# A two-layer hybrid decoder trunk on one core: expert weights in pieces of 1536 columns, and no native float32 product in the small places

## The chip, the cores and the metric

The kernel runs on one core of one Trainium2 chip. The metric is the device time of one execution in microseconds (us). Engines are written as in the profile: PE is the matrix engine (PEld its loading of the stationary operand), DVE the vector engine, ACT the scalar engine, POOL the general-purpose engine, SP the engine whose queue issues the weight loads. A line such as L241 is line 241 of the kernel before.

## What is computed

Two layers over 256 tokens of width 1024, all float32. Each layer adds a mixer (gated delta rule heads, forgetting attention, pooling groups) and then a feed-forward part: dense in layer 0, and in layer 1 two of eight experts for each token. The change is in the last of these:

```
def swiglu(h, w_gate, w_up, w_down):
    return (jax.nn.silu(h @ w_gate) * (h @ w_up)) @ w_down

def moe_swiglu(h, router, w_gate, w_up, w_down):
    ...
    top_p, top_i = lax.top_k(probs, TOP_K)
    ...
    for e in range(N_EXPERTS):
        out = out + gates[:, e:e + 1] * swiglu(ht, w_gate[e], w_up[e], w_down[e])
```

Each expert has w_gate and w_up of 1024 x 1536 and w_down of 1536 x 1024, so 18.87 MB of weights an expert and 151 MB in all.

## The kernel before

The program runs four stages in a row: "mix0", "dense", "mix1" and "all" (the experts). In all of them weights stream from HBM in **pieces** (`piece`, L283): a DMA on SP's queue into a float32 buffer `raw`, a copy on ACT that rounds it to the float32r tile `whi` (L238), a subtraction on DVE that leaves the rest in the float32r tile `wlo` (L241). PE then makes a product of full precision out of several float32r products (`mm3`, L246: high x high, high x low, low x high). A `raw` buffer is free for the next load when DVE has written `wlo`; a pair `whi`, `wlo` is free when PE has made its last product with it.

The buffers are 1152 columns wide (PIECE, L55). Six `raw` buffers (L196) and four pairs (L197) serve all four stages; the expert stage has six more `raw` buffers in its own pool (`load`, L268, and L1329).

The expert stage first normalizes, routes and sorts: the experts get eight **places** by how many tokens they have (`places`). Places 2, 4 and 7 are **small** (SMALL, L41): at most 64 tokens, whose high and low parts lie side by side in the 128 columns of one stationary tile, so that two products (with `whi` and with `wlo`) do what `mm3` does with three. The other five places are **big**, with up to 128 tokens. For each place four **chunks** of 384 expert columns are worked through (`steps`, L1241): `gate_up` (L1151) makes two sums `ps_e` over eight k-blocks of 384 columns, `down` (L1191) transposes the result (`ps_ht`), splits it into `ehi`, `elo` and adds three k-blocks of 1024 columns into `ps_y`. After the last chunk of a place `finish` scales `ps_y` on ACT and DVE (`yh`, `yl`), and after places 1, 3, 5 and 7 `scatter` makes `ps_sc` and adds it to `xs` on DVE. `gather` (L1124) fetches the token columns of the next two places (`ps_ga`, `gThi`, `gTlo`).

A chunk's weights come in nine pieces before: three of gate, three of up (1152, 1152 and 768 columns, by `k_cuts`, L64) and three of down (1024 columns each). In a small place the 768-column piece of gate and of up is not split: `whole` (L277) loads it and PE multiplies the float32 `raw` tile itself, in native float32 (L1161 to L1165). So a small chunk has seven splits and a big one nine.

The order of instructions on each engine is set by the framework's scheduler from the program's priorities; pieces are put 2000 instructions ahead (AHEAD, L56) by `high_priority`. Each engine works through its own order strictly in turn.

Of the kernel before, what the change touches and what calls it, by code (L numbers as in the profile page):

```python
# [16 lines left out]
F32 = mybir.dt.float32  # L17
F32R = mybir.dt.float32r
# [7 lines left out]
D = 1024  # L26
# [9 lines left out]
NFC = 4  # L36
# [15 lines left out]
for _n, _c, _s in GROUPS:  # L52
    GOFF[_n], GCOLS[_n] = _o, _c
    _o += 8 * _c
PIECE = 1152  # L55
AHEAD = 2000  # L56
RING = 6
BANKS = {"mix0": {"A": 3, "D": 3, "F": 2}, "mix1": {"A": 3, "D": 3, "F": 2},
         "dense": {"A": 4, "D": 2, "F": 2}, "all": {"A": 2, "D": 4, "F": 2}}

OUT_ORDER = (3, 4, 5, 6, 7, 0, 1, 2)


def k_cuts(n):  # L64

    step = PIECE // n
    return [(a, min(8, a + step)) for a in range(0, 8, step)]


# [120 lines left out]
class Kernel:  # L190
    def __init__(self, ctx, tc, aps, out, dbg=None):
        self.tc, self.nc, self.d, self.out = tc, tc.nc, aps, out
        self.dbg = dbg
        pool = lambda n, b, **k: ctx.enter_context(tc.tile_pool(name=n, bufs=b, **k))
        self.cp = pool("const", 1)
        self.rp = pool("ring", RING)  # L196
        self.sp = pool("split", 4)  # L197
        self.big = pool("big", 2)
        self.sm = pool("small", 2)
        self.loads = self.more = 0  # L200
        self.guard = None
        self.phase_insts = []

# [61 lines left out]
            self.nc.sync.dma_start(self.dbg[name], ap)  # L265


    def load(self, ap, n):  # L268
        self.loads += 1
        if self.more and self.loads % (RING + self.more) >= RING:  # L270
            raw = self.wk.tile([128, PIECE], F32, tag="raw2", name="raw", bufs=self.more)
        else:
            raw = self.rp.tile([128, PIECE], F32, tag="raw", name="raw")
        self.nc.sync.dma_start(raw[:, :n], ap)
        return raw

    def whole(self, ap):  # L277

        n = ap.shape[1]
        with self.tc.high_priority(offset=AHEAD):  # L280
            return self.load(ap, n)[:, :n]

    def piece(self, ap):  # L283

        n = ap.shape[1]
        with self.tc.high_priority(offset=AHEAD):
            src = self.load(ap, n)[:, :n]
            hi = self.sp.tile([128, PIECE], F32R, tag="whi", name="whi")
            lo = self.sp.tile([128, PIECE], F32R, tag="wlo", name="wlo")
# [819 lines left out]
    def experts(self, over, xh, xl):  # L1109
# [81 lines left out]
        def down(p, fc, hh, py):  # L1191
            small = p in small_ones
# [8 lines left out]
                h1 = wk.tile([128, 3, 128], F32R, tag="ehi", name="ehi", bufs=2)  # L1201
                h2 = wk.tile([128, 3, 128], F32R, tag="elo", name="elo", bufs=2)
            self.hi_lo(h1, h2, ps[:, :3 * r].rearrange("p (j c) -> p j c", j=3))
            for j in range(3):
                wh, wl = self.piece(self.weights(p, fc, 2, j * D, j * D + D))
                for i in range(2):
                    c = slice(i * 512, i * 512 + 512)
                    first, last = fc == 0 and j == 0, fc == NFC - 1 and j == 2
                    if small:
                        x = h[:, j].rearrange("p i c -> p (i c)")  # L1210
                        self.mm(py[i], x, wh[:, c], first, False)
                        self.mm(py[i], x, wl[:, c], False, last)
                    else:
                        self.mm3(py[i], h1[:, j], h2[:, j], wh[:, c], wl[:, c], first, last)

        def finish(p, py):
            sl, tk = info
# [99 lines left out]
            self.store()  # L1317


def build(tc, aps, out, dbg=None, stop=None):  # L1320
    with ExitStack() as ctx:
        k = Kernel(ctx, tc, aps, out, dbg)
        k.setup()
        for name, part in (("mix0", lambda: k.mixer(0)), ("dense", k.dense), ("mix1", lambda: k.mixer(1)), ("all", k.moe)):
            if stop == "setup":
                break
            k.n4 = 10 if name == "all" else 3
            k.banks = BANKS[name]
            k.more = 12 - RING if name == "all" else 0  # L1329
            with tc.tile_pool(name=name, bufs=1) as k.wk, tc.tile_pool(name=name + "_ps", bufs=1, space=PSUM) as k.pp:  # L1330
                part()
            if stop == name:
                break
        if not stop or stop == "all":
            return
        k.store()


# [10 lines left out]
```

## Time and profile before

| what | value |
|---|---|
| median of 3 runs | 986.07 us (984.82 to 990.4) |
| the profiled execution, its own time | 986.57 us |
| its span, first to last instruction | 984.8 us |
| busy share of the span | PE 94%, PEld 84%, DVE 75%, ACT 63%, POOL 13% |
| mean granted PE clock | 0.981 of full speed |
| pieces of expert weights | 128 of 576 KB, 96 of 512 KB, 64 of 384 KB; median 5.8 to 6.0 us from issue to landing |

Busy shares are means over four stages. The expert stage takes the last part of the span: its first product `ps_e` starts at 544 us, the last `wlo` ends at 970.6 us. In the table of windows a stretch is one place, cut at the start of the place's first `wlo` on DVE; each row gives the busy time of the engines in it, with the number of instructions in brackets. A busy PE is modelled from pipelined products, so that back-to-back starts and not the busy time tell whether PE waits.

### The profile page before, as it was taken

The page shows a single profiled execution, that of the slowest core. Times are in us where ns is not written, and L with a number is a line of the kernel's source. Part 1 is how long each engine was busy: PE and PEld are TensorE (multiplying, and loading weights), DVE is VectorE, ACT ScalarE, POOL GpSimd, SP SyncE. Part 2 cuts the span into 40 slices and gives each one's busy share as a digit, 9 for nine tenths or more (in the row PEclk, how much of TensorE's full clock was granted, in tenths as well). Part 3 has the DMA queues.
Part 4 walks back from the last instruction along what each step waited for, and adds up shares of the span by engine and source line. Part 5 has one row for each costly group of instructions (what it writes and reads, how often), then busy time and mean ns, then how long its engine had stood idle before and what let it go on. Part 6 is the DMA issues. An engine that isn't in the chain of part 4 may idle for free.

```text
span 984.8 us, 17576 instructions
## 1 busy us (share of the span) xinstructions
PE 926.0 (94%) x6483; PEld 825.3 (84%) x6483; DVE 733.9 (75%) x1036; ACT 624.0 (63%) x987; POOL 129.3 (13%) x196
## 2 busy tenths in 40 slices
PE   6998998999999989889994999999999899999996
PEld 6987776999999979888773999987899788998874
DVE  5877657655555567857658587999899898998895
ACT  6754545544444457565635388887887688777773
POOL 2596100000000023891002000000000000000000
PEclk9999999999999999999997799999999999999999
DMA  9534113666666637342135299999999999998991
GB/s 353 159 99 129 45 44 126 206 191 190 181 184 191 170 113 234 109 121 76 41 104 210 82 366 323 351 366 370 394 350 378 353 338 363 377 347 320 328 401 49
DMA packets 61983, 224.78 MB, mean 228 GB/s; under 512 B 6896, under 2 KB 7152, under 8 KB 61888
## 3 DMA queue, kind: packets, MB, share of 16 engines
q1 hardware_dynamic: 61344, 221.62, 64.7%
q0 software_dynamic: 544, 1.94, 0.6%
q8 instruction: 53, 0.87, 0.4%
q14 instruction: 42, 0.34, 0.1%
HBM read 222.49 MB, written 1.05 MB: 227 GB/s over the span
## 4 chain that ended last, share of the span: by engine, by line
PE 75%; DVE 9%; POOL 6%; DMA 3%; ACT 2%; issue 2%; SPq 0%; DVEq 0%; ACTq 0%; POOLq 0%
PE ps_e L244 23%; PE ps_gu L244 13%; PE ps_y L244 11%; PE ps_dn L244 6%; PE ps_out L244 4%; DVE wlo L241 3%; DMA raw<-moe 2%; PE ps_ga L244 2%; PE ps_fq L244 2%; PE ps_zabf L244 2%; POOL U L576 2%; PE ps_o L244 1%; PE ps_p L244 1%; POOL tmp L574 1%; PE ps_s L244 1%
## 5 line engine op out<-in xcount | busy, mean ns | idle before, releaser
L241 DVE TENSOR_TENSOR wlo<-raw,whi 128x1024 fp32r<-128x1024 f32 (+3 forms) x394 | 478.7, 1240 | 138.1 <-ACT whi L238 135.1
L238 ACT ACTIVATE whi<-raw 128x1024 fp32r<-128x1024 f32 (+3 forms) x394 | 412.5, 1066 | 185.9 <-PE ps_e L244 51.6
L244 PE MATMUL ps_e<-wlo,gThi 128*128 128x384 f32 x464 | 160.8, 347 | 4.4 <-DVE wlo L241 4.4
L244 PE MATMUL ps_e<-whi,gThi 128*128 128x384 f32 x464 | 156.8, 344 | 1.2 <-ACT whi L238 1.2
L244 PE MATMUL ps_e<-whi,gTlo 128*128 128x384 f32 x320 | 108.0, 339 | 0.0
L244 PE MATMUL ps_gu<-hThi,whi 128*128 128x256 f32 x352 | 99.8, 283 | 1.3 <-DVE hTlo L241 1.3
L244 PE MATMUL ps_gu<-hThi,wlo 128*128 128x256 f32 x352 | 99.4, 283 | 0.0
L244 PE MATMUL ps_gu<-hTlo,whi 128*128 128x256 f32 x352 | 99.4, 282 | 0.0
L244 PEld LDWEIGHTS ps_e<-wlo,gThi 128*128 128x128 f32 x464 | 88.4, 191 | 9.6 <-DVE wlo L241 6.8
L244 PEld LDWEIGHTS ps_e<-whi,gThi 128*128 128x128 f32 x464 | 88.2, 191 | 4.6 <-ACT whi L238 1.6
L244 PE MATMUL ps_y<-wlo,ehi 128*128 128x512 f32 x192 | 73.4, 401 | 1.0 <-DVE wlo L241 1.0
L244 PEld LDWEIGHTS ps_gu<-hThi,whi 128*128 128x128 f32 x352 | 67.3, 191 | 2.5 <-DVE hTlo L241 1.5
L244 PEld LDWEIGHTS ps_gu<-hTlo,whi 128*128 128x128 f32 x352 | 67.3, 191 | 1.0
L244 PEld LDWEIGHTS ps_gu<-hThi,wlo 128*128 128x128 f32 x352 | 67.3, 191 | 0.0
L244 PE MATMUL ps_y<-whi,ehi 128*128 128x512 f32 x192 | 65.7, 407 | 1.3 <-DVE ehi L241 1.3
L244 PEld LDWEIGHTS ps_e<-whi,gTlo 128*128 128x128 f32 x320 | 61.1, 191 | 0.6
L244 PE MATMUL ps_y<-whi,elo 128*128 128x512 f32 x120 | 46.5, 391 | 0.0
L244 PEld LDWEIGHTS ps_y<-whi,ehi 128*128 128x128 f32 x192 | 36.1, 190 | 9.6 <-DVE ehi L241 2.1
L244 PEld LDWEIGHTS ps_y<-wlo,ehi 128*128 128x128 f32 x192 | 36.3, 190 | 9.1 <-DVE wlo L241 1.8
L244 PE MATMUL ps_dn<-whi,fhi 128*128 128x512 f32 x88 | 35.0, 398 | 0.0
L244 PE MATMUL ps_e<-raw,gThi 128*128 128x384 f32 x96 | 34.9, 486 | 0.0
L244 PE MATMUL ps_dn<-wlo,fhi 128*128 128x512 f32 x88 | 34.8, 395 | 0.0
(394 smaller groups left out, 1791.8 us busy)
## 6 DMA issues: line engine op xcount, KB each, us to landing
raw<-moe SPq DMA_DIRECT2D x128, 576.0 KB, 6.0
raw<-moe SPq DMA_DIRECT2D x96, 512.0 KB, 5.9
raw<-ffn SPq DMA_DIRECT2D x66, 512.0 KB, 3.6
raw<-moe SPq DMA_DIRECT2D x64, 384.0 KB, 5.8
raw<-win SPq DMA_DIRECT2D x34, 512.0 KB, 3.7
raw<-wout SPq DMA_DIRECT2D x16, 512.0 KB, 3.6
raw<-win SPq DMA_DIRECT2D x8, 402.0 KB, 5.0
raw<-win SPq DMA_DIRECT2D x4, 576.0 KB, 5.0
```

What stands on the lines that cost most here:

```text
L238: return self.nc.scalar.activation(out, in_, AF.Copy, scale=scale)
L241: return self.nc.vector.tensor_tensor(out, a, b, op=op)
L244: self.nc.tensor.matmul(out, l, r, start=start, stop=stop)
L574: nc.gpsimd.tensor_tensor(tv, nv[:, :, j + 1:16, j:j + 1].to_broadcast(sh), uv[:, :, j:j + 1, 0:j + 1].to_broadcast(sh), op=ALU.mult)
L576: nc.gpsimd.tensor_tensor(u, u, tv, op=ALU.subtract)
```

## The change

Expert weights get buffers of their own: the pools of `raw`, `whi` and `wlo` are opened by `stream` for the first three stages (1152 columns, six `raw`, four pairs) and again for the expert stage (1536 columns, nine `raw`, three pairs). `raw` holds as many columns in the expert stage as before (9 x 1536 = 12 x 1152), and so do the pairs (3 x 1536 = 4 x 1152). A chunk comes in six pieces of 1536 columns: four k-blocks of gate or up each, and for down one and a half k-blocks each. The native float32 products are gone: small places split every piece and make two float32r products of each k-block.

```
-PIECE = 1152
-RING = 6
+PIECES = {False: (1152, 6, 4), True: (1536, 9, 3)}
...
-        self.rp = pool("ring", RING)
-        self.sp = pool("split", 4)
...
-    def load(self, ap, n):
-        self.loads += 1
-        if self.more and self.loads % (RING + self.more) >= RING:
-            raw = self.wk.tile([128, PIECE], F32, tag="raw2", name="raw", bufs=self.more)
-        else:
-            raw = self.rp.tile([128, PIECE], F32, tag="raw", name="raw")
-        self.nc.sync.dma_start(raw[:, :n], ap)
-        return raw
...
+    def stream(self, ctx, experts):
+
+        self.cols, ahead, split = PIECES[experts]
+        name = "e" if experts else ""
+        self.rp = ctx.enter_context(self.tc.tile_pool(name="ring" + name, bufs=ahead))
+        self.sp = ctx.enter_context(self.tc.tile_pool(name="split" + name, bufs=split))
...
-                for k0, k1 in k_cuts(384):
-                    w = self.weights(p, fc, s, k0 * 384, k1 * 384)
-                    if small and k1 == 8:
-
-                        w = self.whole(w)
-                        for k in range(k0, k1):
-                            c = slice((k - k0) * 384, (k - k0 + 1) * 384)
-                            self.mm(ps[:, :384], g[0][:, k, e].bitcast(F32), w[:, c], False, k == 7)
-                        continue
-                    wh, wl = self.piece(w)
+                for k0, k1 in k_cuts(384, self.cols):
+                    wh, wl = self.piece(self.weights(p, fc, s, k0 * 384, k1 * 384))
...
-            for j in range(3):
-                wh, wl = self.piece(self.weights(p, fc, 2, j * D, j * D + D))
-                for i in range(2):
...
+            for j in range(6):
+                j, i = j // 2, j % 2
+                if (2 * j + i) % 3 == 0:
+                    at = (2 * j + i) * 512
+                    wh, wl = self.piece(self.weights(p, fc, 2, at, at + 1536))
...
+        with ExitStack() as weights:
+            k.stream(weights, False)
+            stage("mix0", lambda: k.mixer(0))
+            stage("dense", k.dense)
+            stage("mix1", lambda: k.mixer(1))
+        with ExitStack() as weights:
+            k.stream(weights, True)
+            stage("all", k.moe)
```

Up to the last loads of the second mixer the order of every engine is the same as before. Behind that it differs at the head of the expert stage and inside the chunks.

At the head of the expert stage DVE works on the normalization (`hTlo`, then `nt` and `nr`), the router's result `lg` and its maximum `rmx`, with the first pieces' splits between them. Before:

```order
L241 TENSOR_TENSOR hTlo<-pst,hThi 128x4x128 x4
L241 TENSOR_TENSOR wlo<-raw,whi 128x1152
L241 TENSOR_TENSOR wlo<-raw,whi 128x768
L241 TENSOR_TENSOR wlo<-raw,whi 128x1152
L241 TENSOR_TENSOR nt<-nv,nr 128x2
L241 TENSOR_TENSOR nt<-nt,nr 128x2
L336 TENSOR_SCALAR nt<-nt 128x2
L241 TENSOR_TENSOR nr<-nr,nt 128x2
L241 TENSOR_TENSOR lg<-ps_lg,nr 128x16
L1098 COPY gt_6334<-nr 128x16
L1000 TENSOR_REDUCE rmx<-lg 128x2
```

On DVE at the same place, now:

```order
L239 TENSOR_TENSOR hTlo<-pst,hThi 128x4x128 x4
L239 TENSOR_TENSOR nt<-nv,nr 128x2
L239 TENSOR_TENSOR nt<-nt,nr 128x2
L327 TENSOR_SCALAR nt<-nt 128x2
L239 TENSOR_TENSOR nr<-nr,nt 128x2
L1089 COPY gt_6342<-nr 128x16
L239 TENSOR_TENSOR wlo<-raw,whi 128x1536 x2
L239 TENSOR_TENSOR lg<-ps_lg,nr 128x16
L239 TENSOR_TENSOR wlo<-raw,whi 128x1536
L991 TENSOR_REDUCE rmx<-lg 128x2
```

The three splits have moved from ahead of `nt` to both sides of `lg`, and have 4608 columns in place of 3072 (a fourth split of 1152 columns stood further ahead before). On ACT the two copies `xh`, which POOL's subtractions `xl` need, stand accordingly: the first now ahead of every `whi`, the second behind one, where three `whi` stood ahead of both before; `rt`, which feeds `lg`, has two `whi` ahead of it now. The first load of the stage, which waited for DVE alone before, now waits for the last product of the second mixer on PE too.

On PE inside a small place (`ps_y` of one chunk beside `ps_e` of the next), before:

```order
L244 MATMUL ps_e<-whi,gThi 128x384
L244 MATMUL ps_e<-wlo,gThi 128x384
L244 MATMUL ps_e<-whi,gThi 128x384
L244 MATMUL ps_e<-wlo,gThi 128x384
L244 MATMUL ps_e<-raw,gThi 128x384 x2
L244 MATMUL ps_y_7664<-wlo,ehi 128x512
L244 MATMUL ps_y_7665<-wlo,ehi 128x512
```

On PE in a small place, now:

```order
L242 MATMUL ps_e<-whi,gThi 128x384
L242 MATMUL ps_e<-wlo,gThi 128x384
L242 MATMUL ps_e<-whi,gThi 128x384
L242 MATMUL ps_e<-wlo,gThi 128x384
L242 MATMUL ps_ga<-disp_6183,xl_6175 128x256
L242 MATMUL ps_ga<-disp_6184,xl_6179 128x256
```

The two native products at the end of each sum `ps_e` (four records in the trace, two for each) have become four float32r products.

## Rows read from the trace of the kernel before

**Rows 1.** The page, part 1: engine, busy us (share of the span), instructions.

```profile
PE 926.0 (94%) x6483; PEld 825.3 (84%) x6483; DVE 733.9 (75%) x1036; ACT 624.0 (63%) x987; POOL 129.3 (13%) x196
```

**Rows 2.** The page, part 4: the chain that ended last, shares by engine.

```profile
PE 75%; DVE 9%; POOL 6%; DMA 3%; ACT 2%; issue 2%; SPq 0%; DVEq 0%; ACTq 0%; POOLq 0%
```

**Rows 3.** Windows, one for a place: us, busy us by engine, PEclk, DMA share, GB/s.

```profile
604.41:657.99 53.58, 53.58 (x294) 50.26 (x293) 48.16 (x47) 43.68 (x54) 0.00 (x0) 1.00 0.96 353
657.99:705.99 48.00, 45.82 (x219) 37.36 (x218) 44.81 (x51) 38.84 (x52) 0.00 (x0) 1.00 0.98 368
705.99:760.15 54.16, 54.13 (x297) 49.98 (x296) 47.87 (x48) 44.25 (x59) 0.00 (x0) 1.00 0.99 373
760.15:810.52 50.37, 47.58 (x221) 39.04 (x220) 45.29 (x51) 38.31 (x49) 0.00 (x0) 0.97 0.94 341
...
924.93:970.63 45.70, 42.98 (x195) 33.33 (x195) 43.08 (x47) 36.16 (x46) 0.00 (x0) 1.00 0.75 296
```

**Rows 4.** Windows of place 2, instructions with `wlo` alone: PE, PEld, DVE.

```profile
657.99:705.99 48.00, 25.68 (x71) 13.14 (x70) 34.73 (x28) 1.00 0.98 368
```

**Rows 5.** Windows of two small chunks of place 2, columns as in Rows 3.

```profile
686.53:695.95 9.42, 9.42 (x46) 8.14 (x45) 9.42 (x9) 9.27 (x11) 0.00 (x0) 1.00 0.95 333
695.95:705.99 10.04, 10.04 (x55) 8.32 (x54) 9.91 (x12) 9.14 (x17) 0.00 (x0) 1.00 1.02 410
```

**Rows 6.** Groups by shape, 562 to 985 us: busy us, mean ns | idle before, releasers.

```profile
L241 DVE TENSOR_TENSOR wlo<-raw,whi 128x1152 fp32r<-128x1152 f32 x123 | 163.8, 1352 | 20.4 <-ACT whi L238 18.4 <-DMA raw<-moe 1.3 <-PE ps_y L244 0.2
...
L241 DVE TENSOR_TENSOR wlo<-raw,whi 128x768 fp32r<-128x768 f32 x38 | 36.2, 952 | 1.8 <-ACT whi L238 1.7
...
L241 DVE TENSOR_TENSOR ehh<-ps_e,esg 128x384 f32<-128x384 f32 x20 | 11.1, 554 | 3.1 <-PE ps_e L244 3.1
...
L238 ACT ACTIVATE whi<-raw 128x1152 fp32r<-128x1152 f32 x122 | 139.7, 1164 | 27.9 <-PE ps_e L244 12.8 <-PE ps_y L244 11.3 <-DMA raw<-moe 2.7
...
L238 ACT ACTIVATE whi<-raw 128x768 fp32r<-128x768 f32 x38 | 32.1, 846 | 7.9 <-PE ps_e L244 6.3 <-PE ps_y L244 0.4 <-DMA raw<-moe 0.4
L218 ACT ACTIVATE esg<-ps_e,slot 128x384 f32<-128x384 f32 x19 | 10.8, 567 | 1.9 <-PE ps_e L244 1.9
```

**Rows 7.** Timeline of PE in place 2: start us, us, instruction, count.

```profile
658.36 0.33 PE L244 MATMUL ps_e<-whi,gThi 128*128 128x384 f32 x1
658.54 0.33 PE L244 MATMUL ps_e<-wlo,gThi 128*128 128x384 f32 x1
658.71 1.45 PE L244 MATMUL ps_e<-raw,gThi 128*128 128x384 f32 x4
659.70 0.63 PE L244 MATMUL ps_e<-wlo,gThi 128*128 128x384 f32 x1
660.17 0.34 PE L244 MATMUL ps_e<-whi,gThi 128*128 128x384 f32 x1
```

**Rows 8.** Waits, 560 to 980 us and SP's to 965 us: total us, times, longest.

```profile
ACT whi L238 <- DMA raw<-moe: 3.5, 5, 1.8
...
SPq L274 <- DVE wlo L241: 203.8, 212, 3.8
```

**Rows 9.** Timeline of DVE and POOL at the head of the expert stage.

```profile
526.45 3.50 DVE L241 TENSOR_TENSOR wlo<-raw,whi 128x1152 fp32r<-128x1152 f32 x3
529.86 2.30 DVE L241 TENSOR_TENSOR nt<-nv,nr 128x2 f32<-128x2 f32 x1
532.20 2.26 DVE L241 TENSOR_TENSOR nt<-nt,nr 128x2 f32<-128x2 f32 x1
...
535.17 0.17 DVE L1000 TENSOR_REDUCE rmx<-lg 128x2 f32<-128x16 f32 x1
...
529.23 5.21 POOL L1307 TENSOR_TENSOR xl<-xn,xh 128x1024 fp32r<-128x1024 f32 x2 [13.26 <-ACT nr L218]
```

**Rows 10.** Windows of 2 us in place 4, columns as in Rows 3.

```profile
782.00:784.00 2.00, 0.70 (x4) 0.56 (x5) 2.00 (x4) 0.33 (x1) 0.00 (x0) 0.98 1.01 388
784.00:786.00 2.00, 2.00 (x7) 1.90 (x7) 0.18 (x1) 0.77 (x1) 0.00 (x0) 0.50 1.02 349
```

More of the change, by code (lines that the diff above doesn't have):

```diff
@@ L61, with k_cuts @@
 OUT_ORDER = (3, 4, 5, 6, 7, 0, 1, 2)
-def k_cuts(n):
-    step = PIECE // n
+def k_cuts(n, most=PIECES[False][0]):
+    step = most // n
     return [(a, min(8, a + step)) for a in range(0, 8, step)]
@@ L195, in __init__ @@
         self.cp = pool("const", 1)
-        self.rp = pool("ring", RING)
-        self.sp = pool("split", 4)
         self.big = pool("big", 2)
         self.sm = pool("small", 2)
-        self.loads = self.more = 0
         self.guard = None
@@ L265, in dump @@
             self.nc.sync.dma_start(self.dbg[name], ap)
-    def load(self, ap, n):
-        self.loads += 1
-        if self.more and self.loads % (RING + self.more) >= RING:
-            raw = self.wk.tile([128, PIECE], F32, tag="raw2", name="raw", bufs=self.more)
-        else:
-            raw = self.rp.tile([128, PIECE], F32, tag="raw", name="raw")
-        self.nc.sync.dma_start(raw[:, :n], ap)
-        return raw
[L277 to L281, printed above, removed]
+    def stream(self, ctx, experts):
[3 more added lines that the diff above has]
+        self.sp = ctx.enter_context(self.tc.tile_pool(name="split" + name, bufs=split))
     def piece(self, ap):
@@ L286, in piece @@
         with self.tc.high_priority(offset=AHEAD):
-            src = self.load(ap, n)[:, :n]
-            hi = self.sp.tile([128, PIECE], F32R, tag="whi", name="whi")
-            lo = self.sp.tile([128, PIECE], F32R, tag="wlo", name="wlo")
+            src = self.rp.tile([128, self.cols], F32, tag="raw", name="raw")[:, :n]
+            self.nc.sync.dma_start(src, ap)
+            hi = self.sp.tile([128, self.cols], F32R, tag="whi", name="whi")
+            lo = self.sp.tile([128, self.cols], F32R, tag="wlo", name="wlo")
             parts = self.hi_lo(hi[:, :n], lo[:, :n], src)
@@ L1203, in down @@
             self.hi_lo(h1, h2, ps[:, :3 * r].rearrange("p (j c) -> p j c", j=3))
-            for j in range(3):
-                wh, wl = self.piece(self.weights(p, fc, 2, j * D, j * D + D))
-                for i in range(2):
[L1207 to L1214, printed above, removed]
+            for j in range(6):
[3 more added lines that the diff above has]
+                    wh, wl = self.piece(self.weights(p, fc, 2, at, at + 1536))
+                c = slice((2 * j + i) * 512 - at, (2 * j + i) * 512 - at + 512)
+                first, last = fc == 0 and j == 0, fc == NFC - 1 and j == 2
+                if small:
+                    x = h[:, j].rearrange("p i c -> p (i c)")
+                    self.mm(py[i], x, wh[:, c], first, False)
+                    self.mm(py[i], x, wl[:, c], False, last)
+                else:
+                    self.mm3(py[i], h1[:, j], h2[:, j], wh[:, c], wl[:, c], first, last)
         def finish(p, py):
@@ L1317, in moe, with build @@
             self.store()
-def build(tc, aps, out, dbg=None, stop=None):
+def build(tc, aps, out, dbg=None):
     with ExitStack() as ctx:
@@ L1323, in build, with stage @@
         k.setup()
-        for name, part in (("mix0", lambda: k.mixer(0)), ("dense", k.dense), ("mix1", lambda: k.mixer(1)), ("all", k.moe)):
-            if stop == "setup":
-                break
+        def stage(name, part):
             k.n4 = 10 if name == "all" else 3
             k.banks = BANKS[name]
-            k.more = 12 - RING if name == "all" else 0
             with tc.tile_pool(name=name, bufs=1) as k.wk, tc.tile_pool(name=name + "_ps", bufs=1, space=PSUM) as k.pp:
                 part()
[L1332 to L1336, printed above, removed]
+        with ExitStack() as weights:
[6 more added lines that the diff above has]
+            stage("all", k.moe)
 def kernel(**inputs):
```

## The prediction

> **What bounds the kernel now.** Read the page first: PE is busy 94% of the span and DVE 75% [rows 1], and three quarters of the chain that ended last are PE [rows 2]. Those are means over four stages. Up to the last loads of the second mixer the order of every engine is unchanged, so only the expert stage matters, and it is read by windows, one for each place [rows 3]. The reader should see three things there. In the big places 1 and 3 PE is busy for the whole stretch (53.58 of 53.58, 54.13 of 54.16 us), with DVE some 5 to 6 us short of it: PE is the bound. In the small places 2, 4 and 7 DVE is busy 44.81 of 48.00, 45.29 of 50.37 and 43.08 of 45.70 us, so its idle time is only 3.2, 5.1 and 2.6 us. And inside place 2 there are chunks in which DVE never rests: 9.42 of 9.42 and 9.91 of 10.04 us [rows 5]. So PE and DVE are about level in the small places, and neither may grow.
>
> The DMA share of 0.94 to 0.99 in four of the five looks like a third bound. The waits say otherwise: ACT waited for landings 3.5 us in all, while SP waited 203.8 us, in 212 waits, for DVE to free a `raw` buffer [rows 8]. Loads wait for splits, not splits for loads. But there is little room above: the best chunk moved 410 GB/s [rows 5], at which the 18.87 MB of one place take 46.0 us.
>
> **What the change removes: native products.** In place 2 the four native records start at 658.71 and the next product at 659.70; the one behind it starts 0.47 us later and not 0.175, the step of float32r products in the same rows (658.36, 658.54, 658.71) [rows 7]. That is 0.99 + 0.30 = 1.29 us, for which four float32r products take 0.70. So PE saves 0.59 us on each of 24 sums (three places, four chunks, two sums): 4.7 us a place, 14.1 us in all.
>
> **What it adds: splits in the small places.** The trace has no split of 1536 columns. DVE's take 952 ns at 768 columns and 1352 at 1152 [rows 6], 1.04 ns a column; the straight line gives 1752 ns at 1536. ACT's take 846 and 1164, so 1482. A small place has 28 splits now (16 of 1152 columns and 12 of 1024), on that line 36.3 us, and DVE is busy 34.73 us with them [rows 4]: neighbours overlap by some 0.05 us. 24 splits of 1.70 us are 40.8 us: **+6.0 us of DVE in each small place**, since 768 columns of gate and of up are now split in every chunk. In a big place nine splits a chunk become six of the same columns in all, which saves DVE three fixed parts of 0.15 us (952 less 768 x 1.04); PE is the bound there, so this is worth nothing.
>
> With 6.0 us more, DVE needs 50.8, 51.3 and 49.1 us in places that last 48.00, 50.37 and 45.70. Even if all its idle time were used up they would be longer by 2.8, 0.9 and 3.4 us, 7.1 in sum; if none were, by 18. The idle time is partly handing over between engines (in [rows 10] DVE works through while PE waits), so I take half of it as usable: 18.0 - 5.4 = 12.6. Against this stands PE's gain. Where DVE sets the pace, PE no longer trails by all the pairs it holds, and starts the big place behind a small one earlier. That is possible behind places 2 and 4, by 0 to 4.7 us each; I take half, 4.7 in sum. Behind place 7 comes only the end. Small places: **+7.9 us**, between -2.3 (7.1 - 9.4) and +18.
>
> A rule of the Trainium skill speaks for larger instructions here: Perfetto Trace Analysis, section Optimizing Scalar/DVE Operations, says that grouping work into larger operations can improve throughput if the engine is saturated. The fixed part in the rows agrees (0.15 us a split); by that rule alone DVE would gain 20 big chunks x 0.46 = 9 us, by the rows nothing, since the big places aren't DVE's.
>
> **The ring of pairs.** Three pairs of 1536 hold as many columns as four of 1152, but the loop is tighter. A pair goes through ACT (1.48), DVE (1.75) and PE. A big piece is twelve products, 12 x 0.175 = 2.10 us, so the loop is 5.33 us and three pieces of PE are 6.30: 0.97 us to spare. With 1152 columns it is 1.16 + 1.35 + 1.58 = 4.09 in four pieces of 1.58, that is 2.2 to spare, and PE didn't wait [rows 3]. Once a chunk `esg` (0.567) and `ehh` (0.554) [rows 6] stand in the way, 1.12 us together: 0.15 too much if they hit the same pair, before any handing over. Over 20 big chunks that is 0 to +9 us; near the untroubled rows I take **+2**.
>
> **The head of the stage.** Before, three splits stood ahead of `nt`, in DVE's 3.50 us from 526.45; then POOL's two subtractions held the two tiny `nt` for 2.30 and 2.26 us, and `rmx` came at 535.17 [rows 9]. Now `nt` comes first and meets POOL, whose input ACT copies earlier; two splits of 1.75 stand between `nr` and `lg` and a third between `lg` and `rmx`. The chain through `rmx`, the ranks and the first gather is what the whole stage waits for. The same 4.6 us of POOL and 5.1 us of splits in place of 3.5 give +1.6; `rt` on ACT stands behind two longer copies but is done before DVE asks for it. I take **+2** (-1.5, if the splits fit beside POOL, to +3.5). The first load of the stage now waits for the last reader of the old pairs on PE; the nine loads then go out at once, still ahead of the normalization, and nothing but the splits waits for them. SP's other waits have the same form.
>
> **The sum**, on the profiled execution's own 986.6 us (984.8 of span and 1.8 around it): +7.9 + 2 + 2 = +11.9, so 998.5. That execution is 0.5 above the median of the runs shown: **998.0 us**.
>
> **The rivals.**
>
> *PE's gain counts in full and DVE's splits are hidden: faster.* The small places then last as long as PE or the transfers need: place 2 46.0 (transfers; PE 43.3), place 4 46.0, place 7 41.0, since its weights run out early (296 GB/s). That is -2.0 - 4.4 - 4.7 = -11.1, with the head +2: 977. It needs DVE's 50.8 us to shrink below 46, a 1536-column split of under 1.50 us. Against it stand the two durations that give 1752 and the chunks in which DVE never rests [rows 5]. The Trainium skill, in DMA: Bandwidth & Descriptors, section Bandwidth, bids to batch DMAs to 1 MiB or more; by it pieces of 768 KB would lower the 46.0. No row has such a load, and the waits in [rows 8] say that loads aren't waited for. 0.15.
>
> *All goes into the idle time: no change.* DVE's idle time is used up (+7.1), PE's whole gain behind places 2 and 4 comes back (-9.4), the head costs 2 and the loop nothing: 986. For it speaks that idle time of 5.1 us in place 4 is a wait for PE's own chain; against it, that place 2 has full chunks. 0.25 for anything from 981 to 991.
>
> *The loop binds in the big places.* At +9 in place of +2, and with PE waiting long enough to lose clock: in place 4 the granted clock fell to 0.50, the 1.2 GHz level, right after a stretch in which PE was busy 0.70 of 2 us [rows 10], and the place's mean is 0.97, 1.5 us lost. Two more such falls give 998 + 7 + 3 = 1008. It decides once the two extra instructions meet one pair in each chunk. The Trainium skill's same section on Scalar/DVE operations says that where these engines aren't saturated but cause bubbles on others, breaking up instructions may let work finish sooner. That is this rival; the rows show no bubble in the big places yet. 0.18.
>
> **How the numbers follow.** The forecast (991 to 1004) has 0.42. A measurement of this kernel can tell about 0.5% from no change, 981 to 991. Faster 0.15, same 0.25, slower 0.42 + 0.18 = 0.60. The range reaches from the upper part of the faster case to the loop's: 979 to 1010, leaving out some 0.1 below and 0.07 above.
>
> **What would show it.** Each step has its place in the profile after: PE's products of `raw` gone; `wlo` of 1536 columns at 1.75 us (below 1.5 the first rival wins); small places with DVE busy over 97% and lasting 50 to 53 us; big places still with PE busy throughout, else the loop binds; `rmx` some 2 us later; SP still waiting for `wlo`. If ACT or DVE wait for landings by more than some 10 us in all, the transfers have become the bound and the sum is wrong.

## The result and the profile after

The changed kernel takes 995.78 us (median of 7 runs, 993.79 to 998.06); the kernel before, run beside it, 988.37 us. The ratio is 1.0072, with a 95% interval of 1.0053 to 1.009: slower by 0.7%, or 7.4 us. The forecast was 998.0 with a range of 979 to 1010, and slower had the largest chance. The profiled execution after took 998.06 us (span 996.3), 2.3 us above its median; the one before 986.57, 1.8 below the median of the runs beside it. So the two traces differ by 11.5 us where the medians differ by 7.4. What follows reads places from the traces and prices from the medians.

The page of the kernel after, part 1 (engine, busy us, share of the span, instructions) and the first line of part 4 (the chain that ended last):

```profile
PE 919.6 (92%) x6483; PEld 821.0 (82%) x6483; DVE 746.4 (75%) x964; ACT 629.4 (63%) x915; POOL 129.8 (13%) x196
...
PE 70%; DVE 15%; POOL 7%; ACT 4%; issue 4%; DMA 1%; DVEq 0%; SPq 0%; POOLq 0%; ACTq 0%
```

Against [rows 1] and [rows 2]: PE is busy 6.4 us less and DVE 12.5 us more, and DVE's share of the chain rose from 9 to 15%. The shares of busy time hardly tell anything. The windows do, one for each of the places 1 to 7, cut where DVE starts a place's first split (us; busy us and instructions of PE, weight loads, DVE, ACT and POOL; granted clock; DMA share; GB/s):

```profile
602.79:655.26 52.47, 52.47 (x289) 49.20 (x288) 46.36 (x34) 41.38 (x41) 0.00 (x0) 1.00 0.95 346
655.26:708.77 53.51, 48.11 (x236) 39.88 (x235) 51.39 (x48) 44.34 (x53) 0.00 (x0) 0.97 0.94 357
708.77:762.07 53.30, 51.77 (x280) 47.24 (x280) 46.14 (x35) 41.13 (x42) 0.00 (x0) 1.00 0.95 355
762.07:816.45 54.38, 48.70 (x232) 40.43 (x231) 51.57 (x48) 44.18 (x47) 0.00 (x0) 0.94 0.93 344
816.45:868.72 52.27, 52.01 (x285) 48.01 (x284) 46.14 (x34) 41.76 (x39) 0.00 (x0) 1.00 0.96 364
868.72:928.52 59.80, 58.95 (x326) 54.54 (x325) 49.45 (x40) 41.31 (x39) 0.00 (x0) 1.00 0.91 332
928.52:976.36 47.84, 39.10 (x185) 30.70 (x183) 47.83 (x42) 41.63 (x41) 0.00 (x0) 1.00 0.72 265
```

Beside [rows 3] there are three things to see. Place 2 went from 48.00 to 53.51 us, place 4 from 50.37 to 54.38 and place 7 from 45.70 to 47.84: that is where the time went. DVE is now busy 51.39 of 53.51 and 47.83 of 47.84 us there, and PE only 48 and 39. The big places 1 and 3 are shorter, by 1.1 and 0.9 us, and place 5 by 2.4. Places 3 and 5 stand behind small ones, and PE now starts them with less of the small place left to do; place 1 does not, so the head start can't be its reason. In place 1 PE is busy for all of the 52.47 us, as it was before; in place 3 it now idles 1.5 us. Place 5 before:

```profile
810.52:865.17 54.65, 53.62 (x294) 49.68 (x293) 47.55 (x48) 44.02 (x52) 0.00 (x0) 1.00 0.99 374
```

Chunks of the small places 2 and 7, same columns:

```profile
655.26:667.80 12.54, 12.43 (x64) 10.96 (x63) 12.53 (x11) 12.03 (x13) 0.00 (x0) 1.00 1.00 389
667.80:684.94 17.14, 13.14 (x54) 9.95 (x52) 15.43 (x18) 9.87 (x11) 0.00 (x0) 0.90 0.87 327
...
928.52:941.06 12.54, 12.06 (x60) 9.96 (x59) 12.53 (x11) 12.18 (x13) 0.00 (x0) 1.00 0.93 317
941.06:953.39 12.33, 9.35 (x45) 7.14 (x45) 12.33 (x12) 10.95 (x11) 0.00 (x0) 1.00 1.00 372
```

In three of the four DVE never rests. But ACT stands at 12.03 and 12.18 of 12.54 us right beside it, which the prediction did not weigh. In the second chunk of place 2, 17.14 us long, PE is idle for 4.0 us, and the granted clock of the chunk is 0.90.

The new splits, in the groups by shape from 545 us on (busy us, mean ns, idle before and what ended it):

```profile
L239 DVE TENSOR_TENSOR wlo<-raw,whi 128x1536 fp32r<-128x1536 f32 x189 | 328.1, 1752 | 49.3 <-ACT whi L236 48.2
...
L236 ACT ACTIVATE whi<-raw 128x1536 fp32r<-128x1536 f32 x189 | 279.8, 1488 | 87.9 <-PE ps_e L242 61.6 <-PE ps_y L242 17.8 <-DMA raw<-moe 6.0
```

1752 ns was the prediction's figure, and 1488 stands against 1482. ACT waited for a landing once, for 6.0 us (551 to 557, in place 0). SP still waits for DVE, from 560 to 971 us (total, times, longest), longer than in [rows 8]:

```profile
SPq L278 <- DVE wlo L239: 294.9, 175, 7.0
```

The transfers have not become the bound.

### The profile page after: what moved, and what is told of

It reads as the page before. It is cut to its first block, busy times and chain, and to the rows that moved or that the text cites. A ratio compares the mean times of both kernels' runs of the same rounds, so it can differ in the third digit from the quotient of the medians.

```text
span 996.3 us, 16923 instructions
## 1 busy us (share of the span) xinstructions
PE 919.6 (92%) x6483; PEld 821.0 (82%) x6483; DVE 746.4 (75%) x964; ACT 629.4 (63%) x915; POOL 129.8 (13%) x196
## 4 chain that ended last, share of the span: by engine, by line
PE 70%; DVE 15%; POOL 7%; ACT 4%; issue 4%; DMA 1%; DVEq 0%; SPq 0%; POOLq 0%; ACTq 0%
PE ps_e L242 19%; PE ps_gu L242 13%; PE ps_y L242 9%; DVE wlo L239 8%; PE ps_dn L242 6%; PE ps_out L242 4%; ACT whi L236 2%; PE ps_fq L242 2%; PE ps_ga L242 2%; PE ps_zabf L242 2%; POOL U L567 2%; PE ps_o L242 1%; PE ps_v L242 1%; PE ps_p L242 1%; POOL cacc L505 1%
## 5 line engine op out<-in xcount | busy, mean ns | idle before, releaser
L239 DVE TENSOR_TENSOR wlo<-raw,whi 128x1536 fp32r<-128x1536 f32 (+2 forms) x322 | 492.6, 1542 | 136.3 <-ACT whi L236 134.8
L236 ACT ACTIVATE whi<-raw 128x1536 fp32r<-128x1536 f32 (+2 forms) x322 | 418.9, 1310 | 196.4 <-PE ps_e L242 61.6
L242 PE MATMUL ps_e<-wlo,gThi 128*128 128x384 f32 x512 | 179.3, 350 | 10.4 <-DVE wlo L239 10.0
L242 PE MATMUL ps_e<-whi,gThi 128*128 128x384 f32 x512 | 173.1, 344 | 1.3 <-ACT whi L236 1.1
L242 PEld LDWEIGHTS ps_e<-wlo,gThi 128*128 128x128 f32 x512 | 98.3, 192 | 19.9 <-DVE wlo L239 18.9
L242 PEld LDWEIGHTS ps_e<-whi,gThi 128*128 128x128 f32 x512 | 97.7, 192 | 5.0 <-ACT whi L236 3.7
L242 PE MATMUL ps_y<-wlo,ehi 128*128 128x512 f32 x192 | 76.8, 411 | 1.4 <-DVE wlo L239 1.3
L242 PE MATMUL ps_y<-whi,ehi 128*128 128x512 f32 x192 | 71.2, 412 | 3.8 <-DVE ehi L239 3.2
L242 PE MATMUL ps_dn<-whi,flo 128*128 128x512 f32 x88 | 33.3, 389 | 0.0
```

Of the source, the lines that this page charges most:

```text
L236: return self.nc.scalar.activation(out, in_, AF.Copy, scale=scale)
L239: return self.nc.vector.tensor_tensor(out, a, b, op=op)
L242: self.nc.tensor.matmul(out, l, r, start=start, stop=stop)
```

## The experiments

Each kernel was timed beside the kernel before, in four rounds; the medians of the kernel before were 987.70 (e1 to e4), 988.50 (e5 to e8), 988.53 (e9 to e11) and 988.15 us (e12). The ratios are to it. They are taken from all runs of a round and not from the two medians, from which they differ by up to 0.0011, and their intervals reach 1.3 to 3 us to either side. So a step between kernels of different rounds is uncertain by some 2 us. Such steps are given in medians, with the figure that the ratios give beside it where it matters.

**The two halves of the change, one at a time.** e1 keeps the large pieces and puts native float32 back; the core of its edit (the new number of `piece` is how many columns it splits):

```
-    wh, wl = self.piece(self.weights(p, fc, s, k0 * 384, k1 * 384))
+    wh, wl, w = self.piece(self.weights(p, fc, s, k0 * 384, k1 * 384), 768 if small and k1 == 8 else 1536)
...
+        if small and k >= 6:
+            self.mm(ps[:, :384], g[0][:, k, e].bitcast(F32), w[:, c], False, k == 7)
```

> The changed kernel with one part undone: pieces stay at 1536 columns in nine raw buffers and three pairs, but in the small places the last two 384-column blocks of gate and of up are multiplied in native float32 again, so that 768 columns of the second piece are not split. Theory (the added splits in the small places are the cost): DVE's splits per small place fall from 40.8 us to 16 x 1.70 + 8 x 0.90 = 34.4 us, the three small places go back to about 48, 50 and 46 us, and the time is 985 to 989, level with the kernel before or up to 0.4% faster, since the earlier start of the stage (1.6 us) stays. Rival (coarser pieces and three pairs are the cost): 992 to 996, within 0.4% of the changed kernel.

Measured: 989.31 us, ratio 1.0021 (1.0006 to 1.0036). The theory holds for the splits: 6.5 us of the change's loss (5.0 by the ratios) are gone with them. But e1 isn't faster than before, and in its trace the small places did not go back to 48 and 50 us: places 2 and 4 took 53.4 and 52.7. That trace is of its slowest execution (993.98 us, 4.7 above its median).

e2 keeps the pieces of 1152 columns and splits everything:

```
-    if small and k1 == 8:
-        w = self.whole(w)
-        ...
-        continue
     wh, wl = self.piece(w)
```

> The kernel before with the other part alone: pieces stay at 1152 columns (nine a chunk, twelve raw buffers, four pairs), and the small places split all columns of gate and up; no native product. Theory (added splits): 8 more splits of 768 columns per small place are 8 x 0.90 = 7.2 us of DVE, more than the 6.0 of the changed kernel because of the fixed part of each split; small places +6 to +7 us each, big places behind them 3 to 4 us back in sum, no earlier head: 999 to 1004. Rival (the pieces are the cost): 988 to 991, since PE saves 0.59 us in each of 24 sums and nothing else changes.

Measured: 999.45 us, ratio 1.013 (1.01 to 1.0161), as the theory said. So the split of everything costs 6.5 us with large pieces and 11.8 with small ones, where it takes 36 splits a place and not 24. That e2 is 3.7 us behind the changed kernel (5.7 by the ratios) is not all a merit of the larger pieces: 3.3 of it is the place of the buffers, below.

**The number of pairs.** e3 changes one line:

```
-PIECES = {False: (1152, 6, 4), True: (1536, 9, 3)}
+PIECES = {False: (1152, 6, 4), True: (1536, 7, 4)}
```

> The changed kernel with four pairs of 1536 columns and seven raw buffers in place of three and nine. Theory (three pairs cost nothing, PE never waits in the big places; the fourth split only stands ahead of the adds into xs at the head of the stage): head 1 to 3 us later, the rest the same, 995 to 999. Rival (the loop of three pairs costs in the small places, where PE waits most): 990 to 993. Seven raw buffers in place of nine cost nothing in either, as ACT hardly waits for landings.

Measured: 995.75 us, ratio 1.0075 (1.0049 to 1.01): no difference from the changed kernel. Three pairs cost nothing that can be told. The reason in the expectation was wrong on one point: in its trace the fourth split isn't ahead of the adds into `xs`, it stands after `rmx`.

**The order at the end.** In the changed kernel the last transposes start at 976.98. Timeline of its last splits (start us, us, instruction, idle before and releaser):

```profile
972.48 1.74 DVE L239 TENSOR_TENSOR wlo<-raw,whi 128x1536 fp32r<-128x1536 f32 x1
974.15 0.54 DVE L239 TENSOR_TENSOR ehh<-ps_e,ehh 64x384 f32<-64x384 f32 x1
974.62 1.74 DVE L239 TENSOR_TENSOR wlo<-raw,whi 128x1536 fp32r<-128x1536 f32 x1
976.28 0.54 DVE L239 TENSOR_TENSOR ehh<-ehh,esg 64x384 f32<-64x384 f32 x1
...
976.98 0.55 PE L1179 MATMUL ps_ht<-cst,ehh 64*128 64x64 f32 x3 [3.00 <-DVE ehh L239]
```

The last `ehh` waits behind two splits that PE needs only after it, and PE is idle for 3.00 us. What follows, in windows of 2 us with the columns of above:

```profile
975.00:977.00 2.00, 0.02 (x1) 0.06 (x1) 1.83 (x2) 0.00 (x0) 0.00 (x0) 0.85 0.00 0
977.00:979.00 2.00, 2.00 (x7) 1.41 (x8) 0.36 (x1) 0.33 (x1) 0.00 (x0) 0.50 0.00 0
979.00:981.00 2.00, 2.00 (x6) 1.60 (x5) 0.00 (x0) 0.00 (x0) 0.00 (x0) 0.50 0.03 8
981.00:983.00 2.00, 2.00 (x6) 1.56 (x5) 0.00 (x0) 0.00 (x0) 0.00 (x0) 0.50 0.00 0
```

The granted clock is 0.50, the 1.2 GHz level, for the last sums. e4 makes those two splits depend on the last `ehh` and on `ehi`, in issue order alone:

```
+    if small and p == NE - 1 and fc == NFC - 1:
+        self.dep(self.parts[1], near[at // 1536])      # near: the last ehh, then ehi
```

> The changed kernel with DVE's order changed at one place: in the last chunk of place 7 the two splits of the down weights stand behind the last ehh and behind ehi, not ahead of them. Theory (the last ehh stands behind 3.4 and 1.75 us of splits, PE idles 3 us, and then runs 12 products at half clock): PE's last transposes start at 974 to 974.5 and not at 977, the products behind them run at full clock, the end comes 3 to 5 us earlier: 991 to 993. Rival (the end is DVE's total work in place 7 and the order gives nothing): 995 to 996.

Measured: 993.23 us, ratio 1.0057 (1.0037 to 1.0077), 2.5 us less than the changed kernel (1.5 by the ratios), under the 3 to 5 expected, and with an interval that overlaps. The traces are clearer: from the first split of place 7 to the end of the span it is 67.8 us in the changed kernel and 63.5 in e4. The mechanism:

```profile
971.20 0.55 DVE L239 TENSOR_TENSOR ehh<-ehh,esg 64x384 f32<-64x384 f32 x1
971.67 1.74 DVE L239 TENSOR_TENSOR wlo<-raw,whi 128x1536 fp32r<-128x1536 f32 x1
...
971.98 0.40 PE L1179 MATMUL ps_ht<-cst,ehh 64*128 64x64 f32 x3
```

and the clock behind it is 1.00:

```profile
975.00:977.00 2.00, 2.00 (x10) 1.50 (x8) 0.35 (x1) 0.20 (x1) 0.00 (x0) 1.00 0.00 0
```

**What each engine's work is worth in a small place.** e5 and e10 walk from e1 to the changed kernel engine by engine. In e10 PE does the changed kernel's products, and neither ACT nor DVE has the added work:

```
     if small and k >= 6:
+        c = slice(c.start - 768, c.stop - 768)
-        self.mm(ps[:, :384], g[0][:, k, e].bitcast(F32), w[:, c], False, k == 7)
+        self.mm(ps[:, :384], g[0][:, k, e], wh[:, c], False, False)
+        self.mm(ps[:, :384], g[0][:, k, e], wh[:, c], False, k == 7)
```

In e5 ACT copies all 1536 columns, and only DVE's part is left out (the edit against the changed kernel, cut):

```
-            parts = self.hi_lo(hi[:, :n], lo[:, :n], src)
+            c = cut or n
+            parts = self.hi_lo(hi[:, :n], lo[:, :c], src, c)
...
+        if isinstance(scale, int):
+            return self.copy(hi, src), self.tt(lo, src[:, :scale], hi[:, :scale].bitcast(F32), ALU.subtract)
```

> Pieces of 1536 columns and no native product, but without DVE's added work: in the small places the low part of the last two 384-column blocks of gate and of up is not made, and the product that would take it takes the high part a second time, so PE does the changed kernel's work and DVE that of e1_native_in_1536. (The low parts of these blocks are missing from the sums.) It prices the two sides alone: against e1 only the native products differ, against the changed kernel only the splits. Theory A (PE's gain counts only in part, since DVE's 34 us of splits and its other 10 us are near the length of a small place): 983 to 987, so native products cost 2 to 6 of the 14.1 us that PE spends more on them. Theory B (PE's gain counts in full once DVE is relieved, the first rival of the prediction): 975 to 980.

> As e5_neither, with ACT relieved as well: in the small places neither the high nor the low part of the last two blocks of gate and up is made, and their products take the high part of the two blocks ahead of them twice (those blocks' weights are missing from the sums). PE does the changed kernel's work, DVE and ACT do that of e1_native_in_1536. Theory A (in e5 ACT's added copies, 24 x 0.64 = 15.4 us, ate PE's gain; three engines are level in the small places): 983 to 986. Theory B (PE's time doesn't count in the small places, whatever the others do): 988 to 990.

Measured: e10 987.34 us, ratio 0.9992 (0.997 to 1.0014); e5 989.30 us, ratio 1.0001 (0.9984 to 1.0018). In medians the walk reads: e1 to e10, PE spends 14.1 us less on products (the prediction's price): -2.0. e10 to e5, ACT copies 24 x 0.64 = 15.4 us more: +2.0. e5 to the changed kernel, DVE splits 19.2 us more: +6.5. The ratios give -2.9, +0.9 and +7.0. The first two steps are of the size of their intervals, and no more than their order of size should be read from them; the last is clear of its own. Both theories of e5 were wrong on the time, and e10 came out between its two.

Place 2 in the traces of e1, e10 and e5, one row each:

```profile
657.68:711.05 53.37, 50.12 (x228) 40.38 (x226) 46.58 (x48) 39.78 (x49) 0.00 (x0) 0.94 0.89 342
```

```profile
655.06:706.14 51.08, 46.73 (x229) 40.11 (x227) 46.14 (x48) 39.34 (x49) 0.00 (x0) 0.93 0.94 364
```

```profile
654.94:705.75 50.81, 45.84 (x229) 38.95 (x227) 46.23 (x48) 43.45 (x49) 0.00 (x0) 0.97 0.96 367
```

With DVE as light as in e1, no engine fills the place in e10 and e5: DVE is busy 46 of 51 us, PE 46 to 47, ACT 39 in e10 and 43 in e5. One reading is that the three pass each pair on in a ring, so that an engine that is given less to do mostly waits longer. It is argued from the rows, and two things speak against its simple form: in e10 ACT has 12 us to spare and the place is no shorter than in e5, and a fourth pair in the ring gave nothing in e3, nor in e12 below. The granted clock is below 1.00 in all three, and where it is below, PE's relief is partly lost again; that this is the whole reason isn't shown.

**Relief of DVE.** e6 takes an add of 0.54 us a chunk from DVE. Both halves of up are multiplied by a silu that stands on both halves, and the transpose adds them:

```
-    nc.tensor.transpose(ps[:, j * r:j * r + r], hh[:, j * 128:j * 128 + 128], self.ident[:r, :r])
+    if small:
+        self.mm(ps[:, j * r:j * r + r], hh[:, j * 128:j * 128 + 128], self.fold)   # two identities, stacked
```

> The changed kernel with DVE relieved of one of its other operations in the small places: the two halves of up (products of the high and of the low rows) are no longer added on DVE; both are multiplied by a silu that ACT writes on both halves, and the transpose on PE adds them (a product with two stacked identities). DVE loses one add of 0.54 us in each of 12 chunks, 6.5 us in all; ACT's work stays the same but for 0.1 us a chunk. Theory (DVE sets the length of the small places): 4 to 6.5 us off the changed kernel, 989 to 992. Rival (ACT, 96% busy in the first chunk of a small place, or the hand-overs set it): 994 to 996.

Measured: 995.48 us, ratio 1.0073 (1.0056 to 1.0091), where 989 to 992 was expected; the rival was right on the time. Which of its two causes it is, ACT or the handing over between engines, was not separated. Place 2 in its trace:

```profile
654.53:707.51 52.98, 48.63 (x243) 41.09 (x242) 49.65 (x44) 45.18 (x51) 0.00 (x0) 0.97 0.93 355
```

and its splits on DVE there, with the idle time before them and its releaser:

```profile
L239 DVE TENSOR_TENSOR wlo<-raw,whi 128x1536 fp32r<-128x1536 f32 x24 | 41.3, 1748 | 3.6 <-ACT whi L236 3.6
```

DVE's 1.7 us less gave 0.5 us; it now idles 3.6 us behind ACT's copies in this place, 2.4 in the changed kernel. DVE never rests in three of the four chunks above, and yet it was not alone at the bound.

> The kernel before with the add in the transpose alone: DVE loses 0.54 us in each of 12 chunks of the small places. Theory (DVE and PE are about level there): a third to a half of 6.5 us, 984.5 to 986. Rival (PE is the bound with native products): 987 to 988.5, no change.

The same edit in the kernel before: 987.75 us, ratio 0.9983 (0.9961 to 1.0006), as its rival said: no difference that can be told.

> A candidate for the best: 1536-column pieces with native products as in e1_native_in_1536, the last two splits behind the last ehh as in e4_last_hidden_first, and the add in the transpose as in e6_fold_in_transpose. Theory (the three are independent, DVE in the small places at some 42 us): e1's 989.3 less 2.5 and less 1 to 4: 983 to 986, faster than before by 0.2 to 0.5%. Rival (with native products PE is the bound of the small places, and relief of DVE gives nothing): 986.5 to 988.

e1 with the edits of e4 and e6: 986.52 us, ratio 0.9974 (0.9957 to 0.9991). It is 2.8 us under e1 in medians, about what e4 gave alone, but 4.7 by the ratios, where e4 gave 1.5; so whether the add in the transpose gave anything here can't be told. It beats both kernels by a little.

**The place of the buffers.** The dense stage isn't touched by the change, and its instructions stand in the same order, yet it ran faster after. Windows from 200 to 350 us in it, before and then after; what counts is the number of products in 150 us at a clock of 1.00:

```profile
200.00:350.00 150.00, 150.00 (x1051) 140.15 (x1051) 83.43 (x106) 66.94 (x89) 0.00 (x0) 1.00 0.61 182
```

```profile
200.00:350.00 150.00, 150.00 (x1076) 141.58 (x1076) 85.65 (x108) 68.04 (x90) 0.00 (x0) 1.00 0.62 186
```

DVE's 22 instructions `flo` stand from the head of the stage to its end (durations in ns, first and last start in us; before, after, and e9, which follows):

```profile
L241 DVE TENSOR_TENSOR flo<-hh,fhi x22: 417/418/424, 186.0 to 357.4; 128x256 fp32r<-128x256 f32 x22
L239 DVE TENSOR_TENSOR flo<-hh,fhi x22: 416/419/426, 185.5 to 353.6; 128x256 fp32r<-128x256 f32 x22
L241 DVE TENSOR_TENSOR flo<-hh,fhi x22: 417/419/426, 185.9 to 354.1; 128x256 fp32r<-128x256 f32 x22
```

That is 171.4 us before and 168.1 us after. What the change does to the stage is to open the pools of the ring and the pairs later, so that they lie behind the activations in SBUF. e9 is the kernel before with that alone; in its trace DVE, ACT and POOL run the same instructions in the same order:

```
-        self.rp = pool("ring", RING)
-        self.sp = pool("split", 4)
         self.big = pool("big", 2)
         self.sm = pool("small", 2)
+        self.rp = pool("ring", RING)
+        self.sp = pool("split", 4)
```

> The kernel before with one thing changed: the ring and the pairs are placed in SBUF behind the activations and not ahead of them, as in the changed kernel; every engine's instructions and their order stay the same. In the profiles the steps of the dense stage's products, which the change doesn't touch, are 119.5 and 233.8 ns before and 117.8 and 226.7 ns after, and the stage (from hh 20 rows in to the last flo) takes 171.1 us before and 167.8 us after. Theory (where the buffers lie sets the step of the products): dense stage 167.8 us, big place 1 down from 53.6 to 52.5 us, in all 984 to 986, a gain of 3 to 5 us that the changed kernel also has and that hides as much of its loss. Rival (drift between executions, or another cause in the change): dense stage 171 us, 988 to 989.

Measured: 985.19 us, ratio 0.9969 (0.9945 to 0.9993), 3.3 us less than before, as the theory said. The same window of its trace:

```profile
200.00:350.00 150.00, 150.00 (x1077) 141.61 (x1076) 85.36 (x109) 68.04 (x90) 0.00 (x0) 1.00 0.62 185
```

and a group of down products in that window, whose mean of 390 ns was 397 before:

```profile
L244 PE MATMUL ps_dn<-whi,fhi 128*128 128x512 f32 x72 | 28.0, 390 | 0.0
```

The `flo` take 168.2 us in e9. In all the traces they take 171.4 with the pools in the old order (before, e2, e8) and 168.1 to 168.3 in the new one, so the gain is no accident of one execution. The changed kernel carries these 3.3 us, which have nothing to do with its pieces, and what the pieces and the splits cost is 995.8 less 985.2, or 10.6 us (10.2 by the ratios). Place 1 did not follow the expectation: 53.45 us in e9, where 52.5 was expected. Its gain in the changed kernel has another cause.

> A candidate for the best: the kernel before with the placement of e9_before_layout and the add in the transpose of e8_before_fold. If the two are independent: e9 less 0 to 1.5 us, 983 to 985.5, faster than before by 0.3 to 0.5%; if the fold gives nothing, as e9.

e9 with the add in the transpose: 983.55 us, ratio 0.9947 (0.9923 to 0.9971). This is the best version found, 0.5% faster than before and 1.2% faster than the changed kernel. Against e9 alone it is 1.6 us, within their intervals.

**What the larger piece costs by itself.** With the buffers placed alike, e1 is 4.1 us slower than e9 (5.1 by the ratios, and their intervals do not meet), though the products are the same and DVE splits the same columns. Place 2 in e9, to set beside e1's row above:

```profile
654.41:702.26 47.85, 45.62 (x218) 37.13 (x218) 44.80 (x52) 38.78 (x52) 0.00 (x0) 1.00 0.97 364
```

Between these two traces e1 is 5.5 us longer in place 2, 2.5 in place 4 and 2.2 from place 7 to the end, with a granted clock of 0.94 in places 2 and 4 against 1.00 and 0.97, and 2.9 us shorter in places 1, 3 and 5. They show where the loss lies, not its size: e1's execution is 4.7 us above its median, e9's 2.8 below.

> e1_native_in_1536 with four pairs and seven raw buffers in place of three and nine. With the same placement of the buffers, e1 (989.3) is 4.1 us slower than e9_before_layout (985.2), although PE does the same products and DVE's splits are equal: that is what the larger pieces cost by themselves. Theory A (the loop of three pairs, the prediction's second term, costs in the small places, where pieces are shared by fewer products): 985 to 987. Theory B (it is the size of a piece: the first product of a chunk waits for a copy and a split of 1.48 + 1.75 us and not 1.16 + 1.35 us, whatever the number of pairs): 988.5 to 990.

Measured: 989.85 us, ratio 1.0013 (1.0 to 1.0027), no better than e1. It is not the number of pairs. So the loss comes with the larger pieces, in the small places and at the end; the expectation's reason, the longer copy and split ahead of a chunk's first product, was not tested by itself. At the end of the kernel e4 gave 2.5 us back by order alone, so a part of the 4.1 may be order.

## Why the prediction came out as it did

**The sum.** It said +11.9 us; measured is +7.4. The forecast time of 998.0 is only 2.2 us too high because the kernel before, too, came out 2.3 us later beside the changed one (988.37) than in the three runs that the prediction had (986.07). On equal placement of the buffers the medians say +10.6, so most of what the sum has too much is one gain that it missed. The rest are terms whose errors cancel in part: the closeness of 10.6 to 11.9 is luck.

**Small places, +7.9.** The runs give +6.5 (e1 to the changed kernel). The direction, the place and the 1752 ns were right. The working was wrong in its parts. DVE's 18 us were counted at 12.6 and cost 6.5 (e5; 7.0 by the ratios); PE's gain was counted at 4.7 and was worth 2 to 3 (e10); ACT's 15.4 us of added copies were counted at nothing, and cost 1 to 2, if anything. The weak step is "PE and DVE are about level", from which every us of DVE beyond half its idle time was made a us of the place. e6, where 6.5 us less of DVE work gave nothing that can be told, shows that DVE's work does not turn into time one for one. That ACT is the third at the bound is argued. Of the signs that the prediction named, `wlo` at 1.75 us was met; places 2 and 4 lasted longer than the 50 to 53 us (53.5 and 54.4), with DVE busy 96 and 95% and not over 97. In the traces the small places lose more, 5.5 + 4.0 us in places 2 and 4 and 7.9 from the start of place 7 to the end, and the big places 1, 3 and 5 give 4.4 back; the head start was foreseen at 4.7, but the 1.1 us at place 1, which no small place precedes, are not it, and show that the cut itself may move with the pieces.

**The clock in the small places** is part of it. After, windows in place 4:

```profile
784.00:786.00 2.00, 0.40 (x3) 0.26 (x3) 2.00 (x3) 0.33 (x1) 0.00 (x0) 0.82 0.95 353
786.00:788.00 2.00, 1.98 (x6) 1.99 (x7) 2.00 (x6) 0.00 (x0) 0.00 (x0) 0.50 0.99 353
788.00:790.00 2.00, 2.00 (x6) 1.71 (x6) 0.43 (x2) 1.48 (x1) 0.00 (x0) 0.50 0.85 341
790.00:792.00 2.00, 2.00 (x6) 1.52 (x6) 1.61 (x1) 1.21 (x1) 0.00 (x0) 0.50 0.06 25
```

Behind a stretch in which PE was busy 0.40 of 2 us the clock is at 0.50, for 6 us here; in [rows 10] it fell in the same way behind 0.70 of 2. The means of the places after are 0.97 and 0.94, and (1 - 0.97) x 53.5 + (1 - 0.94) x 54.4 = 4.9 us; before only place 4 lost some, 1.5. So up to 3.4 of the 9.5 us by which places 2 and 4 grew are clock. The prediction spoke of this only for the big places, in its third rival. It belonged in the small ones, where adding to DVE makes PE wait.

**The ring of pairs, +2.** It came to next to nothing: PE is busy 52.47 of 52.47 us in place 1, it idles 1.5 us in place 3 and 0.3 in place 5 (0.0 and 1.0 before), and four pairs change nothing in e3 and e12. The third rival, the loop binding in the big places, falls with it.

**The head of the stage, +2.** Measured between the second add into `xs` and the first `ps_e` of the experts: 30.27 us before, 30.59 after, +0.3, less than the spread of the traces with the old order there (30.3 to 31.6). `rmx`, which was to come 2 us later, came at 533.62 in place of 535.17. The step that failed took the splits in front of `nt` as the only ones. One split of before stood further ahead, among the adds into `xs`. DVE before, and then after (the first row of each holds the first and second add):

```profile
513.57 1.28 DVE L241 TENSOR_TENSOR xs<-xs,ps_out 128x512 f32<-128x512 f32 x2 [2.09 <-PE ps_out L244]
...
519.54 1.36 DVE L241 TENSOR_TENSOR wlo<-raw,whi 128x1152 fp32r<-128x1152 f32 x1 [2.67 <-ACT whi L238]
520.82 0.68 DVE L241 TENSOR_TENSOR xs<-xs,ps_out 128x512 f32<-128x512 f32 x1
...
511.69 1.29 DVE L239 TENSOR_TENSOR xs<-xs,ps_out 128x512 f32<-128x512 f32 x2 [2.13 <-PE ps_out L242]
...
516.96 0.69 DVE L239 TENSOR_TENSOR xs<-xs,ps_out 128x512 f32<-128x512 f32 x1 [0.47 <-PE ps_out L242]
```

After, the first load of the stage comes too late for that, the third add starts 2.0 us earlier behind the second, and so most of what the longer splits and POOL cost behind it (`nt` at 523.28 for 2.36 us) is given back.

The stretch ahead, from the last `flo` to the second add, is not in the sum, and it is 156.7 us before and 158.7 after. Over the traces it is 156.7 to 157.6 in the five kernels with the old expert stage, at a granted clock of 0.967 to 0.989, and 157.5 to 159.3 in the nine with the new one, at 0.957 to 0.978. DVE and ACT run it in an order that the change leaves alone, and the place of the buffers is not the reason (157.1 in e9); why it is slower was not found.

**Not in the sum: what the larger pieces cost with native products kept, +4.1** (e9 to e1). The two terms of +2 that were wrong in their place had this size together, by chance. The Trainium skill, in Perfetto Trace Analysis, section Optimizing Scalar/DVE Operations, says that where these engines aren't saturated but cause bubbles on others, breaking up instructions may let work finish sooner. The runs agree: with native products kept, where DVE is busy 46.58 of 53.37 us in e1's place 2, the same columns in larger instructions made the kernel slower. That bubbles on PE are the way by which they did is argued. The same section of the Trainium skill says that grouping can help a saturated engine, and that fits too: with everything split, e2 on the better placement would stand at some 996.2 (999.45 less 3.3, an estimate from e9; 998 by the ratios), no faster than the changed kernel, so there the 12 splits fewer in each small place seem to have made up for the 4.1 us.

**The rivals.** PE's gain in full would have needed a split below 1.50 us; it took 1.75, and e10 shows that even with the added splits and copies away PE's gain is worth 2 to 3 us and not 11. All going into idle time failed with e5 to the changed kernel. That the loads would profit from larger pieces was open by the Trainium skill's rule in DMA: Bandwidth & Descriptors, section Bandwidth, to batch to 1 MiB or more: place 2 moved 357 GB/s with 768 KB pieces, 368 before, and SP's loads waited 294.9 us for buffers, so nothing here shows a gain from it.

## What to carry to other kernels

Before pricing work that is moved from one engine to another, read from the stage's windows how close the third engine is, and do not take a us of an engine's work for a us of time: here a us added on DVE cost a third of itself (6.5 of 19.2), and one removed next to nothing (e6). A change that reorders the pools also moves buffers, so compare a stage that the change does not touch first; a difference there is not the change's idea. Look at the last few instructions on the engine that feeds the end: a split that nobody needs yet, in front of the result that everybody waits for, cost its own length here and then the clock (e4).

## What the runs showed that was not expected

The place of the operands in SBUF changed the pace of float32r products here: the same instructions in the same order took a mean step of 119.5 ns (256 columns) and 233.8 ns (512 columns) in the dense stage with the ring ahead of the activations, and 117.8 and 226.7 ns with it behind them. Which of the buffers, and what about its address, does it was not tried.

The time of one and the same kernel goes with its clock. The ten runs of e7 reach from 980.52 us at a mean granted clock of 0.984 to 988.03 at 0.975, and the medians of the clock are 0.976 to 0.978 for the kernel before, by round, and 0.971 for the changed one. Part of every comparison here is therefore likely to be how often the clock falls behind a wait of PE, and that part does not show in a sum of durations.
